# Moving one product of the second gate/up pair ahead, and fixing the place of the token scale's sum, in a float32 decoder layer on one core

## The chip, the cores and the metric

The kernel runs on one NeuronCore of a Trainium2 chip. The metric is device time in microseconds (us) for one execution, lower is better; the value given for a kernel is the median of several runs. One core works here, so no other core's work disturbs it.

## The reference

One hybrid decoder layer in float32, with 512 tokens, a model width of 2048 and 16 learned meta tokens in front. What the change touches is its last third:

```python
h = h + o @ w_out[l]                       # o: attention and convolution groups, each normalized
n2 = _rmsnorm(h, g_ffn[l])                 # one scale for each token, from the sum of h*h over 2048
h = h + (jax.nn.silu(n2 @ w_gate[l]) * (n2 @ w_up[l])) @ w_down[l]    # D_FF = 5632
```

`_rmsnorm` multiplies each token by `rsqrt(mean(h*h) + 1e-6)` and each channel by its gain.

## The kernel before, in words

Everything is stored transposed: channels on the 128 partitions, tokens along the free axis. A float32 product is made of three fp32r products: each operand is split into a high part (a cast on ScalarE, ACT) and a low part (a subtraction on VectorE, DVE), and hi·hi + hi·lo + lo·hi is summed in PSUM (L740 to L742 for the stage in question).

**The stages.** First come the input projection, attention and convolution, then the output projection `w_out` (16 output tiles, L821 to L902), then 44 *pairs* of gate and up tiles (`for f in range(FT)`, L972), then the down projection in four chunks. The change lies where `w_out` ends and the first two gate/up pairs run.

**A pair.** `pair_product` (L744) multiplies the activation, cut into 2 x 2 blocks (token halves by channel halves), with a 2 x 2 arrangement of weight blocks b11, b12, b21, b22 by Winograd's form of Strassen's scheme: seven block products instead of eight. Each product is 8 channel tiles times 3 passes, so 24 matmuls of 128x128 by 128x256. I call them slots 0 to 6:

| slot | weight | activation | PSUM bank |
|---|---|---|---|
| 0 | b11 | f0 | x |
| 1 | t1 = b11 + b12 | f1 | z |
| 2 | t2 = t1 + b22 | f2 | x |
| 3 | b22 | f3 | z |
| 4 | t3 = b12 + b22 | f4 | x |
| 5 | b21 (the product "a12 b21") | f5 | y |
| 6 | t2 + b21 | f6 | x |

"P1s5" below is slot 5 of the second pair, counted from 0. The pair P0 runs its slots in the order 5, 0, 1, 2, 3, 4, 6 (`FIRST_ORDER`, L663), because f5 is ready first; all other pairs run 0 to 6. The banks x, y and z exist twice, so two pairs can be open at once. Where products of different banks have no dependence, the scheduling layer mixes their matmuls, so PE's order is not quite the program's.

**Weights.** `prepare_pair` (L665) makes one split per product, in the order of use. `split_quad` (L639) casts the high part on ACT (L642) and makes the low part on DVE (L643), in a ring of three places of `sw_split`: the split for a product can begin when the product three before it is done. The same function makes the sums: t1 and t3 with `add_quads` (L649), t2 at L686, its last addition at L659 (`add_last`). Sums and raw blocks lie in six places of `sw_in`: places 0 to 3 hold the four loaded blocks, 4 and 5 hold t1/t2 and t3. Once a block is no more needed, the block of the same name of the next pair is loaded over it by SyncE's DMA queue (SP; `load_next`, L616, issued at L614). During `w_out` only places 0 to 3 are used (`load_wide`, L628).

**Activations.** Each finished `w_out` tile goes through `residual` (L835: two multiplications by token scales on DVE, two additions) and a copy with the FFN gain on ACT (L840); then the blocks f0 to f6 are mixed and split (L187, L188, L847 to L852). f0, f1, f2 and f5 stay in SBUF. f3, f4 and f6 find no room until `w_out`'s inputs are released, so they are gathered in DRAM and come back with six DMAs from GpSimd's queue (POOL, L884): f3 in two halves, f4 in two, f6 in two. Between f3's and f4's issues POOL adds the last tile's squares to `acc_h` (L207).

**The token scale of the FFN.** `token_scale` (L493) splits `acc_h`, sums it over the partitions by two products with a matrix of ones (L501 and L502, tile `ss_h`), adds and scales on DVE (L503), and takes the reciprocal root: logarithm and exponential on ACT (L194, L195), then four operations of a Newton step on POOL (L196 to L199), which write the scale back to `acc_h`. It is handed to pair 0 as `fourth` and called behind slot 3 (L773), at a high priority, so that the scheduling layer may move its instructions ahead. `gate` (L938) uses the scale on DVE: L941 for u, L943 for g.

Of the kernel before, what the change touches and what calls it, by code (L numbers as in the profile page):

```python
# [16 lines left out]
D = 2048  # L17
# [16 lines left out]
def hybrid_layer(ctx: ExitStack, tc: tile.TileContext, xT, w_in, w_out, w_gu, w_down, vecs, out):  # L34
# [9 lines left out]
    nc = tc.nc  # L44
    ve, sc, gp, pe = nc.vector, nc.scalar, nc.gpsimd, nc.tensor
# [48 lines left out]
    ones_r = keep.tile([P, P], F32R, name="ones_r")  # L94
# [125 lines left out]
    acc = accs[0]  # L220
# [269 lines left out]
    for h in range(HEADS):  # L490
        head(h)

    def token_scale(acc, dst, count, name, work, eng=ve):  # L493

        sh, sl, v, y, t = work
        split(sh, sl, acc, eng)
        ps = small(f"ss_{name}")  # L500
        pe.matmul(ps, ones_r, sh, start=True, stop=False)  # L501
        pe.matmul(ps, ones_r, sl, start=False, stop=True)  # L502
        ve.tensor_scalar(v, ps, 1.0 / count, EPS, ALU.mult, ALU.add)  # L503
        rsqrt(dst, v, SEQ, y, t, eng)
# [15 lines left out]
    for j in range(HEADS):  # L520
# [5 lines left out]
        y = t512(SEQ, "e2", 2)[:, :SEQ]  # L526
# [101 lines left out]
    def load_wide():  # L628

        i = len(wide)  # L630
        q = ORDER[(i + 2) % 4]
        if i < WIDE:
            wide.append(quad_place(0, q))
            nc.sync.dma_start(wide[i], w_out[OUT_TILES[1 + i // 2], i % 2])
        else:
            wide.append(None)
            load_quad(0, q)

    def split_quad(src, n):  # L639
        k = len(split_w) % (S_AHEAD + 1) * 2  # L640
        hi, lo = (w_place(sw_split, n, k + i) for i in range(2))
        sc.copy(hi, src)  # L642
        ve.tensor_tensor(lo, src, hi.bitcast(F32), ALU.subtract)  # L643
        split_w.append((hi, lo))
# [15 lines left out]
        load_next(i, "21")  # L660


    FIRST_ORDER = (5, 0, 1, 2, 3, 4, 6)  # L663

    def prepare_pair():  # L665
        if len(split_w) < WIDE:
            with tc.high_priority():
                split_quad(wide[len(split_w)], 8)
                load_wide()
            return  # L670
        i, s = divmod(len(split_w) - WIDE, 7)
        if i == len(pairs):
            return
        n = pairs[i][0]
        if i == 0:
            s = FIRST_ORDER[s]
        with tc.high_priority():
            b = {q: quads[i, q] for q in ("11", "12", "21", "22") if (i, q) in quads}
            if s == 0:
                split_quad(b["11"], n)  # L680
                add_quads(i, "t1", b["11"], b["12"])
                load_next(i, "11")
            elif s == 1:
                split_quad(sums["t1"], n)
                sums["t2"] = sums["t1"]
                ve.tensor_tensor(sums["t2"], sums["t2"], b["22"], ALU.add)  # L686
                if i:
                    add_t3(i, b)
            elif s == 2:
                split_quad(sums["t2"], n)  # L690
                if not i:
                    add_t3(i, b)
            elif s == 3:
                split_quad(b["22"], n)
                load_next(i, "22")
            elif s == 4:
                split_quad(sums["t3"], n)
            elif s == 5:
                split_quad(b["21"], n)
                if i:  # L700
                    add_last(i, b)
            else:
                if not i:
                    add_last(i, b)
                split_quad(sums["t2"], n)
                if i + 1 == SIX:
                    load_quad(SIX + 1, QUADS[1])
# [16 lines left out]
    def block_product(ps, act, start):  # L724

        prepare_ahead(1 + S_AHEAD)  # L730
        i = (used[0] - WIDE) // 7
        hi, lo = split_w[used[0]]
        used[0] += 1
        m = ps.shape[-1] // T2
        n = pairs[i][0] // m
        for j in range(m):
            p, skip = ps[:, j * T2 : (j + 1) * T2], m > 1 or not start
            for k in range(n):
                kk = slice((j * n + k) * P, (j * n + k + 1) * P)
                pe.matmul(p, hi[:, kk], act[:, 0, k], start=start and j == k == 0, stop=False, skip_group_check=skip)  # L740
                pe.matmul(p, hi[:, kk], act[:, 1, k], start=False, stop=False, skip_group_check=skip)  # L741
                pe.matmul(p, lo[:, kk], act[:, 0, k], start=False, stop=k == n - 1, skip_group_check=skip)  # L742

    def pair_product(acts, c1, c2, fourth=None):  # L744

        i, cols = (used[0] - WIDE) // 7, c1.shape[-1]

        def bank(name):
            return xyz.tile([P, 512], F32, tag=name, name=f"{name}{i}")[:, :cols]

        def side(name):
            n = {"p1": 0, "p5": 1, "u2": 2}[name]
            if cols == T2 or not n:
                return sides[:, n * T2 : n * T2 + cols]
            return c2[:, 2 - n]

        y, z, x = bank("y"), bank("z"), bank("x")  # L760
        p1, p5, u2 = side("p1"), side("p5"), side("u2")
        if not i:
            block_product(y, acts[5], True)
        block_product(x, acts[0], True)
        sc.copy(p1, x)
        block_product(z, acts[1], True)
        sc.copy(p5, z)
        block_product(x, acts[2], False)
        sc.copy(u2, x)
        block_product(z, acts[3], False)  # L770
        ve.scalar_tensor_tensor(c2[:, 0], z, -1.0, u2, ALU.mult, ALU.subtract)
        if fourth:
            fourth()  # L773
        block_product(x, acts[4], False)
        ve.scalar_tensor_tensor(c2[:, 1], x, -1.0, p5, ALU.mult, ALU.subtract)
        if i:
            block_product(y, acts[5], True)
        ve.tensor_tensor(c1[:, 0], y, p1, ALU.add)
        block_product(x, acts[6], False)
        return x  # L780
# [22 lines left out]
    acts = {}  # L803
# [3 lines left out]
    fx = {i: dram.tile([P, 2, 8, T2], F32R, name=f"fx{i}") for i in (3, 4, 6)}  # L807
    for _ in range(4):
        load_wide()

    def wide_tmp(tag, dt=F32, bufs=1):
        n_tmp[0] += 1
# [8 lines left out]
    for i, j in enumerate(OUT_TILES):  # L821
# [6 lines left out]
        ps = ps_out[i]  # L828
# [75 lines left out]
    acts = [acts[s] for s in range(7)]  # L904
# [211 lines left out]
```

## Time and profile before

| what | value |
|---|---|
| median of 3 runs | 2065.69 us (2063.52 to 2066.52) |
| the profiled execution | 2066.56 us |
| its span | 2064.8 us |
| TensorE (PE) busy | 2051.6 us |
| VectorE (DVE) busy | 1628.3 us |
| ScalarE (ACT) busy | 1016.9 us |
| GpSimd (POOL) busy | 369.3 us |
| gate/up pairs start on PE at | 792.69 us |

How to read it: times of the trace are microseconds from the span's start; the profiled execution's own time is 1.8 us more than its span. In a timeline each row is start, duration, engine, line, operation, output<-input, shape, count, and in brackets the engine's idle time before it and what ended that. Matmuls overlap by their pipeline, so a matmul's cost is the distance from its start to the next one's start, not its duration; the same holds in small for DVE and ACT. "PEclk" is the share of TensorE's full clock that was granted.

### The profile page before, as it was taken

To read this page: it belongs to the slowest core of one execution; us is meant where nothing else is said; L and a number is where in the kernel's file an instruction comes from. 1 tells how busy PE (TensorE), PEld (TensorE's weight loads), DVE (VectorE), ACT (ScalarE), POOL (GpSimd) and SP (SyncE) were. 2 spreads that over 40 slices of the span, in tenths; PEclk is the share of its full clock that TensorE was granted. 3 is DMA by queue.
4 is the path that set the end of the run, shared out by engine and by line. 5 is a ranking of instruction groups with operands and counts; after the bars stand their busy time and mean duration, and the time that the engine had idled before them with its cause. 6 is when DMAs were issued, how large, how long until landed. Compare 5 with 4: busy or idle time off the path is not lost.

```text
span 2064.8 us, 39370 instructions
## 1 busy us (share of the span) xinstructions
PE 2051.6 (99%) x16086; PEld 1977.9 (96%) x16086; DVE 1628.3 (79%) x2133; ACT 1016.9 (49%) x1522; POOL 369.3 (18%) x499
## 2 busy tenths in 40 slices
PE   9999999999999999999999999999999999999999
PEld 8899999999998888999999999999999999999999
DVE  7877767433336668999898898898888888888888
ACT  7666565322224334555455555555555544444443
POOL 0111111010103544111111111011011243121110
PEclk9999999999999999999999999999999999999999
DMA  5122222222335656546545555455455899798864
GB/s 198 63 81 74 81 72 83 82 93 94 98 107 168 187 178 229 159 138 194 169 136 176 159 152 172 148 172 161 147 175 155 256 332 348 195 293 213 217 150 94
DMA packets 144117, 330.41 MB, mean 160 GB/s; under 512 B 12400, under 2 KB 62064, under 8 KB 143936
## 3 DMA queue, kind: packets, MB, share of 16 engines
q1 hardware_dynamic: 67456, 212.50, 32.2%
q0 software_dynamic: 76480, 115.40, 21.8%
q8 instruction: 126, 2.06, 0.4%
q14 instruction: 55, 0.45, 0.1%
HBM read 260.74 MB, written 67.11 MB: 159 GB/s over the span
## 4 chain that ended last, share of the span: by engine, by line
PE 95%; DVE 2%; DMA 2%; ACT 1%; issue 0%; POOL 0%; DVEq 0%; POOLq 0%; ACTq 0%
PE x L740 11%; PE x L741 11%; PE x L742 11%; PE z L740 6%; PE z L741 6%; PE z L742 6%; PE y L742 3%; PE y L740 3%; PE y L741 3%; PE po L719 3%; PE po L721 3%; PE po L720 3%; PE pv L173 2%; PE pu L177 1%; PE pc L173 1%; PE pu L173 1%
## 5 line engine op out<-in xcount | busy, mean ns | idle before, releaser
L642 ACT CAST sw_split<-sw_in 128x1024 fp32r<-128x1024 f32 (+1 forms) x534 | 526.5, 987 | 553.0 <-PE z L741 166.2
L643 DVE TENSOR_TENSOR sw_split<-sw_in,sw_split 128x1024 fp32r<-128x1024 f32 (+1 forms) x534 | 614.6, 1151 | 97.4 <-ACT sw_split L642 94.2
L741 PE MATMUL x<-f,sw_split 128*128 128x256 f32 x1408 | 388.4, 276 | 2.9 <-DMA f<-fx 2.7
L740 PE MATMUL x<-f,sw_split 128*128 128x256 f32 x1408 | 388.5, 276 | 0.2 <-ACT f L187 0.2
L742 PE MATMUL x<-f,sw_split 128*128 128x256 f32 x1408 | 387.9, 276 | 0.0
L741 PEld LDWEIGHTS x<-f,sw_split 128*128 128x128 f32 x1408 | 265.1, 188 | 3.5 <-DMA f<-fx 3.1
L740 PEld LDWEIGHTS x<-f,sw_split 128*128 128x128 f32 x1408 | 265.0, 188 | 1.0 <-ACT f L187 0.4
L742 PEld LDWEIGHTS x<-f,sw_split 128*128 128x128 f32 x1408 | 265.0, 188 | 0.0
L142 DVE TENSOR_TENSOR wlo<-raw,whi 128x512 fp32r<-128x512 f32 (+1 forms) x198 | 139.7, 709 | 125.0 <-ACT whi L141 124.2
L932 POOL DMA_DIRECT2D fd<-s x147 | 103.9, 928 | 684.1 <-DVE s L188 667.6
L141 ACT CAST whi<-raw 128x512 fp32r<-128x512 f32 (+1 forms) x198 | 121.1, 614 | 180.8 <-PE pu L175 64.5
L741 PE MATMUL z<-f,sw_split 128*128 128x256 f32 x704 | 193.7, 275 | 0.2 <-DVE f L188 0.2
L740 PE MATMUL z<-f,sw_split 128*128 128x256 f32 x704 | 193.6, 275 | 0.0
L742 PE MATMUL z<-f,sw_split 128*128 128x256 f32 x704 | 193.6, 275 | 0.0
L649 DVE TENSOR_TENSOR sw_in<-sw_in 128x1024 f32<-128x1024 f32 (+1 forms) x144 | 164.5, 1142 | 4.6 <-DMA sw_in<-w_down 0.6
L742 PE MATMUL x<-ring,sw_split 128*128 128x256 f32 x608 | 167.3, 275 | 0.5 <-DVE sw_split L643 0.5
L740 PE MATMUL x<-ring,sw_split 128*128 128x256 f32 x608 | 167.2, 275 | 0.0
L741 PE MATMUL x<-ring,sw_split 128*128 128x256 f32 x608 | 167.2, 275 | 0.0
L741 PEld LDWEIGHTS z<-f,sw_split 128*128 128x128 f32 x704 | 132.2, 188 | 0.4 <-DVE f L188 0.4
L742 PEld LDWEIGHTS z<-f,sw_split 128*128 128x128 f32 x704 | 132.2, 188 | 0.0
L740 PEld LDWEIGHTS z<-f,sw_split 128*128 128x128 f32 x704 | 132.2, 188 | 0.0
L742 PEld LDWEIGHTS x<-ring,sw_split 128*128 128x128 f32 x608 | 114.1, 188 | 0.7 <-DVE sw_split L643 0.7
(345 smaller groups left out, 5255.9 us busy)
## 6 DMA issues: line engine op xcount, KB each, us to landing
sw_in<-w_gu SPq DMA_DIRECT2D x176, 512.0 KB, 4.1
raw<-w_in SPq DMA_DIRECT2D x92, 512.0 KB, 3.3
fd<-s POOLq DMA_DIRECT2D x147, 256.0 KB, 5.4
sw_in<-w_down SPq DMA_DIRECT2D x96, 384.0 KB, 4.1
ring<-fd POOLq DMA_DIRECT2D x42, 768.0 KB, 17.0
sw_in<-w_out SPq DMA_DIRECT2D x30, 512.0 KB, 3.6
out_T<-d POOLq DMA_DIRECT2D x54, 256.0 KB, 4.6
sw_in<-w_down SPq DMA_DIRECT2D x16, 512.0 KB, 7.8
```

Of the source, the lines that this page charges most:

```text
L141: sc.copy(hi[:, :c], raw)
L142: ve.tensor_tensor(lo[:, :c], raw, hi[:, :c].bitcast(F32), ALU.subtract)
L173: pe.matmul(ps, wh, ah[:, a:b], start=k == 0, stop=False)
L642: sc.copy(hi, src)
L643: ve.tensor_tensor(lo, src, hi.bitcast(F32), ALU.subtract)
L649: return ve.tensor_tensor(sums[name], a, b, ALU.add)
L719: pe.matmul(ps, hi[:, kk], ah, start=k == 0, stop=False)
L720: pe.matmul(ps, hi[:, kk], al, start=False, stop=False)
L740: pe.matmul(p, hi[:, kk], act[:, 0, k], start=start and j == k == 0, stop=False, skip_group_check=skip)
L741: pe.matmul(p, hi[:, kk], act[:, 1, k], start=False, stop=False, skip_group_check=skip)
L742: pe.matmul(p, lo[:, kk], act[:, 0, k], start=False, stop=k == n - 1, skip_group_check=skip)
L932: gp.dma_start(fd[c][s][:, :, k], t[:, :, i])
```

## The change

Pair 1's slot 5 (a12 b21) is made right behind pair 0's slot 5, so P0s5, P1s5, P0s0, P0s1, P0s2, P0s3, P0s4, P0s6, then P1s0 to P1s4 and P1s6; from pair 2 on the order is as before. Its y bank waits in the second y buffer until pair 1 adds it. Its weight block is loaded once more, early, into place 5 of `sw_in` (`load_early`, while `w_out` starts), since b21 of pair 1 is needed again for t2 + b21 and is loaded for that as before. So one 512 KB load is added, and no matmul, split or sum is added or dropped. Since place 5 is taken until P1s5's split, pair 0's sum t3, which goes there, comes behind that split. The second part: the first of the two products with ones of `ss_h` is kept in program order, behind P0s3.

```diff
-        pe.matmul(ps, ones_r, sh, start=True, stop=False)
+        first_sum = pe.matmul(ps, ones_r, sh, start=True, stop=False)
+        if in_order:
+            tc.keep_in_program_order(first_sum)
...
-    FIRST_ORDER = (5, 0, 1, 2, 3, 4, 6)
+    EARLY = 2
+    order_w = [(i, 5) for i in range(EARLY)] + [
+        (i, s) for i in range(len(pairs)) for s in range(7) if i >= EARLY or s != 5
+    ]
+
+    def load_early():
+        quads["early"] = w_place(sw_in, 8, 5)
+        nc.sync.dma_start(quads["early"], pairs[1][1][2])
...
-        if i == 0:
-            s = FIRST_ORDER[s]
+        i, s = order_w[len(split_w) - WIDE]
...
-                split_quad(b["21"], n)
-                if i:
+                split_quad(quads["early"] if i == 1 else b["21"], n)
+                if i >= EARLY:
                     add_last(i, b)
             else:
-                if not i:
+                if i < EARLY:
                     add_last(i, b)
                 split_quad(sums["t2"], n)
...
-        y, z, x = bank("y"), bank("z"), bank("x")
+        y, z, x = early.pop(i, None) or bank("y"), bank("z"), bank("x")
         if not i:
             block_product(y, acts[5], True)
+            early[1] = bank("y", 1)
+            block_product(early[1], acts[5], True)
         block_product(x, acts[0], True)
...
-        if i:
+        if i >= EARLY:
             block_product(y, acts[5], True)
...
     for _ in range(4):
         load_wide()
+    load_early()
...
-            token_scale(acc_h, acc_h, D, "h", (w[:, 0], w[:, 1], a[:, 0], a[:, 1], b), gp)
+            token_scale(acc_h, acc_h, D, "h", (w[:, 0], w[:, 1], a[:, 0], a[:, 1], b), gp, True)
```

More of the change, by code (lines that the diff above doesn't have):

```diff
@@ L491, in hybrid_layer, with token_scale @@
         head(h)
-    def token_scale(acc, dst, count, name, work, eng=ve):
+    def token_scale(acc, dst, count, name, work, eng=ve, in_order=False):
         sh, sl, v, y, t = work
@@ L670, in prepare_pair @@
             return
-        i, s = divmod(len(split_w) - WIDE, 7)
-        if i == len(pairs):
+        if len(split_w) - WIDE == len(order_w):
             return
+        i, s = order_w[len(split_w) - WIDE]
         n = pairs[i][0]
-        if i == 0:
-            s = FIRST_ORDER[s]
         with tc.high_priority():
@@ L730, in block_product @@
         prepare_ahead(1 + S_AHEAD)
-        i = (used[0] - WIDE) // 7
+        i = order_w[used[0] - WIDE][0]
         hi, lo = split_w[used[0]]
@@ L742, in block_product, with bank @@
                 pe.matmul(p, lo[:, kk], act[:, 0, k], start=False, stop=k == n - 1, skip_group_check=skip)
+    n_pair, early = [0], {}
     def pair_product(acts, c1, c2, fourth=None):
-        i, cols = (used[0] - WIDE) // 7, c1.shape[-1]
-        def bank(name):
+        i, cols = n_pair[0], c1.shape[-1]
+        n_pair[0] += 1
+        def bank(name, i=i):
             return xyz.tile([P, 512], F32, tag=name, name=f"{name}{i}")[:, :cols]
```

## The prediction

> **What bounds the kernel now.** I read the page first, then PE's waits around the change, then PE's timeline there, then the engines that release it.
>
> ```profile
> PE 2051.6 (99%) x16086; PEld 1977.9 (96%) x16086; DVE 1628.3 (79%) x2133; ACT 1016.9 (49%) x1522; POOL 369.3 (18%) x499
> ...
> L642 ACT CAST sw_split<-sw_in 128x1024 fp32r<-128x1024 f32 (+1 forms) x534 | 526.5, 987 | 553.0 <-PE z L741 166.2
> ```
>
> PE is busy for 99% of the span, so an edit pays only where PE really waits or runs slowly. PE's waits between 792 and 847 us (columns: total us, times, longest us):
>
> ```profile
> PE x L741 <- DMA f<-fx: 2.7, 2, 2.3
> PE y L742 <- DVE sw_split L643: 1.9, 1, 1.9
> ```
>
> Two waits: for f4 and f6 coming back from DRAM (2.3 and 0.4), and for the low part of P1s5's own split (1.9). Now PE's timeline; the rows are the starts of P0s5; P0s4 with its wait; the wait inside P0s6; P1s3; P1s5; and, as a mark I call M, the first matmul of P2s2 (slot 2 of pair 2). Up to M both kernels issue the same matmuls; from M on both have the same order in the built programs.
>
> ```profile
> 792.69 0.28 PE L740 MATMUL y<-f,sw_split 128*128 128x256 f32 x1
> ...
> 808.40 0.28 PE L740 MATMUL x<-f,sw_split 128*128 128x256 f32 x1
> 810.99 0.39 PE L741 MATMUL x<-f,sw_split 128*128 128x256 f32 x1 [2.32 <-DMA f<-fx]
> ...
> 818.47 0.39 PE L741 MATMUL x<-f,sw_split 128*128 128x256 f32 x1 [0.42 <-DMA f<-fx]
> ...
> 827.47 0.28 PE L740 MATMUL z<-f,sw_split 128*128 128x256 f32 x1
> ...
> 830.19 0.28 PE L740 MATMUL y<-f,sw_split 128*128 128x256 f32 x1
> ...
> 846.26 0.28 PE L740 MATMUL x<-f,sw_split 128*128 128x256 f32 x1
> ```
>
> P1s3 to P1s5 is 830.19 - 827.47 = 2.72 us: one product, 0.1133 a matmul. From P0s5 to M lie 16 products and the two of `ss_h` (0.23 each, estimated as twice 0.1133): 16 x 2.72 + 0.46 = 44.0 of work in 846.26 - 792.69 = 53.6 us. So 9.6 us are lost here, and that is the most the change could win. Where: 15.71 instead of 13.83 (five products and one of `ss_h`) up to P0s4: 1.9, small waits for f0 to f2; 2.5 between P0s4's first two matmuls; then a slow stretch:
>
> ```profile
> 813.00:815.00 2.00, 2.00 (x11) 2.00 (x11) 0.00 (x0) 0.00 (x0) 0.00 (x0) 0.50 1.13 422
> ```
>
> The granted clock is 0.50 here: 11 matmuls in 2 us instead of 18. It follows PE's 2.3 us of waiting, lasts about 3.4 us and so costs 1.7. Then 0.6 at 818.47, 2.1 at P1s5, and crumbs.
>
> **The change part by part.** I compare two limits at M: PE behind f6's landing, and DVE behind the token scale. The later one is the forecast.
>
> *PE behind f6.* f6's second half released PE at 818.47. In the old order PE then stood in P0s6 with 17 matmuls of P1s0 already done. In the new order P0s4, five matmuls of P1s0, then P0s6 follow each other, so at f6's landing 24 matmuls (P1s5) more and 12 of P1s0 fewer are done: 210 matmuls are left before M against 222. 210 x 0.1133 = 23.8, M at 842.3, if nothing else waits: **4.0 us** less. f4's wait goes (PE reaches P0s4 about 2.7 us of work later, f4 lands at 810.99), but what is late next is f6: PE arrives near 815.5 and waits until 818.5. The 2.3 us of waiting at f4 are thus mostly moved, not removed. P1s5's own wait of 2.1 goes, since that product was made long before.
>
> *Does f6 land when it did?* It is issued by POOL behind L207, and shares the DMA engines with SP's weight loads.
>
> ```profile
> 797.96 2.25 POOL L207 TENSOR_TENSOR acc_h<-acc_h,w 128x512 f32<-128x512 f32 x1 [3.34 <-ACT w L206]
> 800.16 2.88 POOL L884 DMA_DIRECT2D f<-fx  x4
> ...
> 824.59 2.14 POOL L199 TENSOR_TENSOR acc_h<-work_a,work_b 128x512 f32<-128x512 f32 x1
> ```
>
> ```profile
> f<-fx POOLq DMA_DIRECT2D x2, 1024.0 KB, 14.5
> ```
>
> ```profile
> DMA packets 1396, 5.10 MB, mean 399 GB/s; under 512 B 95, under 2 KB 95, under 8 KB 1396
> ```
>
> ```profile
> 789.32 3.65 SPq L614 DMA_DIRECT2D sw_in<-w_gu  x2
> ```
>
> L207 waits for the last tile's residual on DVE. Its timeline:
>
> ```profile
> 786.99 2.30 DVE L649 TENSOR_TENSOR sw_in<-sw_in 128x1024 f32<-128x1024 f32 x1
> ...
> 791.41 1.21 DVE L643 TENSOR_TENSOR sw_split<-sw_in,sw_split 128x1024 fp32r<-128x1024 f32 x1
> 792.96 0.69 DVE L836 TENSOR_TENSOR w<-po,acc_a 128x512 f32<-128x512 f32 x1 [0.34 <-PE po L721]
> 793.57 0.68 DVE L838 TENSOR_TENSOR w<-po,acc_c 128x512 f32<-128x512 f32 x1
> ...
> 798.65 0.42 DVE L849 SCALAR_TENSOR_TENSOR src<-src 128x256 f32<-128x256 f32 x1
> 799.10 1.39 DVE L851 SCALAR_TENSOR_TENSOR src<-src 128x256 f32<-128x256 f32 x1
> ...
> 807.74 1.21 DVE L649 TENSOR_TENSOR sw_in<-sw_in 128x1024 f32<-128x1024 f32 x1
> 808.87 1.21 DVE L643 TENSOR_TENSOR sw_split<-sw_in,sw_split 128x1024 fp32r<-128x1024 f32 x1
> ...
> 836.67 1.23 DVE L643 TENSOR_TENSOR sw_split<-sw_in,sw_split 128x1024 fp32r<-128x1024 f32 x1
> ```
>
> At 791.41 stood P0s0's split; in the new order P1s5's stands there, and t3's sum, which ran at 786.99 in idle time, comes behind it, since P1s5's block occupies its place. A sum or a split of 128x1024 takes 808.87 - 807.74 = 1.13 us. So L836 starts at 791.41 + 2 x 1.13 = 793.7 instead of 792.96, and L207 and the issues of f4 and f6 come 0.7 later. SP's load of P1's b12 (789.32, released by t3's sum) moves to 793.7, that of b11 (the second issue of that row, 792.6, released by P0s0's split) to about 796.7: 1.0 MB falls among f3's transfers. At 399 GB/s that is 2.6 us at most if nothing gives way; against it P1's b21 and b22 load later, and P2's b11 no longer ahead of f6's end (0.5 MB, 1.3 us sooner). Bounds for f6's landing: 1.3 earlier to 0.7 + 2.6 = 3.3 later; I take no shift, in the middle of them, because the engines move the same bytes by the same end.
>
> *DVE behind the token scale.* In the old run the second product of `ss_h` starts at 816.60:
>
> ```profile
> L502 PE MATMUL ss_h<-work_r,ones_r x1: 401/401/401, 816.6 to 816.6; 128*128 128x512 f32 x1
> L503 DVE TENSOR_SCALAR work_a<-ss_h x1: 683/683/683, 817.7 to 817.7; 128x512 f32<-128x512 f32 x1
> ```
>
> L503 follows at 817.7. POOL's last step, L199 above, ends at 824.59 + 2.14 = 826.7, so 10.1 after it; the low part of P2s0 follows on DVE at 836.67. In the new order the second product stands 9 matmuls behind P0s3's end. When does P0s3 end? PE's own pace gives 792.69 + 6 x 2.72 = 809.0. But the splits are late: behind the residual (0.75 later) come P0s1's low part, then t2's sum (which was ahead of it), then P0s2's. In order: L836 793.7, two more of 0.6 (793.57 - 792.96), P0s0's low part 1.13 to 796.6, L839 to 797.2, then the copy with the gain on ACT:
>
> ```profile
> 796.62 0.73 ACT L840 ACTIVATE src<-w,vec 128x512 f32<-128x512 f32 x1 [2.91 <-DVE w L839]
> ```
>
> That makes 798.0, and the six mixing operations that follow on DVE, 0.34 each (the distance to the next start is less than the 0.42 shown), end at 800.1. A DVE operation beside POOL's L207 is held up: 799.10's took 1.39, its sibling before it 0.42. The cost of that is 0 to 1.0; I take 1.0.
>
> So P0s1's low part is made from 801.2 to 802.3; PE wants it at 792.69 + 3 x 2.72 + 0.23 = 801.1 and waits 1.2. f2's low part 0.34, t2's sum 1.13: 803.8; ACT's cast of t2 (987 ns in the mean, first row above) to 804.8, low part to 806.0: PE, which could begin P0s2 at 804.9 and use the low part 0.23 later, waits 0.9 more. P0s3 ends near 811.3, or 812.2 if POOL holds up one more operation; both waits lie ahead of the f6 wait, which hides them from PE's limit. The second product of `ss_h` is then at 811.3 to 812.2 plus 1.25: 813.0, 3.6 earlier than now. DVE's L503 is queued behind P1s0's low part, up to 815.2, so 2.2 behind the product instead of 1.1; the chain from L503 to POOL's end, 826.7 - 817.7 = 9.0, gives 824.2.
>
> L941 waits there for the scale, and behind it on DVE stand, up to and with P2s0's low part, eight splits and sums of 1.13, four operations of 0.60 and two of 0.34: 12.1 us, 836.3. That is two splits or sums more than in the old order, where P1s5's split stood behind the scale but three others stood ahead of it. P2s0's third matmul, the first to use that low part, therefore starts at 836.3, and 70 matmuls later is M: 836.3 + 7.9 = 844.2, **2.0 us** earlier than 846.26. This is the later limit, so the forecast.
>
> *Other edits.* The extra 512 KB load is issued at the start of the `w_out` stage:
>
> ```profile
> sw_in<-w_out SPq DMA_DIRECT2D x30, 512.0 KB, 3.6
> ```
>
> Loads like it land in 3.6 us while the product pair that consumes two of them takes 10.9 (48 matmuls of 0.23); if that cover were gone it would cost 0.5 MB at 399 GB/s, 1.3. Ordering the first product with ones behind P0s3 removes no matmul; its cast on ACT is made earlier than needed. Nothing after M changes place, and I find no wait of PE there that grows with an earlier arrival.
>
> The Trainium skill's page "TensorE: Matmul & The Clock Gate", section "HAM oscillation — how this bites in real kernels", warns of idle gaps of more than about 3.4 us. Here a wait of 2.3 us was followed by the halved clock, so the trace shows it for shorter ones. By the page the new f6 wait of about 3 would leave the clock alone, and rival 1 below would keep its whole 4.0; by the row it can halve the clock, and rival 1 keeps 2.3.
>
> **The rivals.**
>
> *1. DVE is not the later limit.* If POOL's chain ends 2 us sooner, only PE's limit counts: 4.0 us less. For it: PE, not DVE, is 99% busy. Against: L941 blocks everything behind it on DVE. A halved clock behind the f6 wait would take 1.7 of it (2.3 left); in the forecast it would hide under DVE's limit, 842.3 + 1.7 = 844.0 against 844.2.
>
> *2. f6 lands later.* With 3.3 us later, PE's limit is 845.6: 0.7 less than before. For it: the engines are busy through 803 to 816. Against: the same bytes in all.
>
> *3. Slower: the token scale comes later, not earlier.* Place: P0s1 and P0s2, where PE waits for splits twice in 5 us. If that halves the clock (1.7) and POOL holds up two more DVE operations (1.0 each), the second `ss_h` product moves by 3.7, and M with it: 844.2 + 3.7 = 847.9, 1.7 slower. It decides from 2.0 us of extra lateness at P0s3's end. For it: DVE has no idle time from 791 to 811. Against: 2.3 us in one piece was needed for the one halving seen.
>
> **How the numbers follow.** The sum stands against the profiled execution, 2066.56: 2066.56 - 2.0 = 2064.6. The median of the runs is 2065.69, 0.87 lower, so the forecast for a median is 2065.69 - 2.0 = 2063.7. Chances: forecast (1 to 3 less) 0.45; rival 1 (3 to 4.5 less, 2061.7 at 4.0) 0.20; rival 2 (0 to 1 less, 2065.0) 0.17; rival 3 (up to 3 more, 2067.4) 0.18. The range 2061.2 to 2066.8 reaches from just past rival 1 to the milder half of rival 3; about 0.05 is left out below and 0.12 above. A measurement of this kernel can tell about 0.2%, 4.1 us, from no change. Faster by that is the far end of rival 1 (0.07); slower by that is the far end of rival 3, with a second halving of the clock (0.04); within it lies the rest, 0.89.
>
> **What would show it.** Right: no wait for f4 at P0s4, one wait of 2 to 3.5 us for f6 in P0s6, small waits for splits at P0s1 and P0s2, second `ss_h` product near 813, POOL's L199 ending near 824, DVE idle ahead of L955 (the old L941), a short wait at P2s0. Wrong: f6 released before 816 or after 820; `ss_h` after 815; PE waiting after M where it did not; more than 5 us between the two kernels' distance from P0s5 to M.

## The result, and the profile after

The changed kernel takes 2066.66 us (median of 22 runs, 2066.06 to 2069.16), the kernel before, run beside it, 2064.31 (22 runs, 2062.82 to 2066.52). The ratio is 1.0013 with a 95% interval of 1.0007 to 1.0019: about 2.4 us slower, where 2.0 less was forecast. The forecast time of 2063.7 stood on the median of three runs, 2065.69; the 22 runs put the kernel before 1.4 lower.

The profiled execution of the changed kernel is the slowest of its 22: 2069.16 us, span 2067.5. PE's share and the costliest group on its page are what they were:

```profile
PE 2051.9 (99%) x16086; PEld 1978.5 (96%) x16086; DVE 1627.6 (79%) x2133; ACT 1017.0 (49%) x1522; POOL 368.4 (18%) x499
...
L644 ACT CAST sw_split<-sw_in 128x1024 fp32r<-128x1024 f32 (+1 forms) x534 | 526.7, 988 | 551.2 <-PE z L749 163.2
```

PE's waits between 785 and 850 us (total, times, longest):

```profile
PE x L748 <- ACT sides L778: 2.7, 1, 2.7
PE x L750 <- DVE sw_split L645: 2.2, 2, 1.8
PE z L750 <- DVE sw_split L645: 1.1, 1, 1.1
```

No wait for f4 or f6 is left. In their place PE waits 2.7 us for a *copy on ACT*, and for splits. PE's timeline shows where: P0s1's low part, P0s2's first matmul, the first product with ones, P1s2's low part.

```profile
803.24 0.38 PE L750 MATMUL z<-f,sw_split 128*128 128x256 f32 x1 [1.07 <-DVE sw_split L645]
...
808.70 0.39 PE L748 MATMUL x<-f,sw_split 128*128 128x256 f32 x1 [2.66 <-ACT sides L778]
...
815.93 0.39 PE L501 MATMUL ss_h<-work_r,ones_r 128*128 128x512 f32 x1
...
829.80 0.39 PE L750 MATMUL x<-f,sw_split 128*128 128x256 f32 x1 [1.79 <-DVE sw_split L645]
```

P0s2 adds into bank x, and ACT's copy of p1 (L778) must have read that bank first. ACT's timeline tells why the copy is late:

```profile
804.75 1.05 ACT L644 CAST sw_split<-sw_in 128x1024 fp32r<-128x1024 f32 x1 [1.95 <-DVE sw_in L694]
806.82 0.62 ACT L187 CAST work_r<-acc_h 128x512 fp32r<-128x512 f32 x1 [1.02 <-DMA f<-fx]
807.34 1.04 ACT L644 CAST sw_split<-sw_in 128x1024 fp32r<-128x1024 f32 x1
808.29 0.37 ACT L778 COPY sides<-x 128x256 f32<-128x256 f32 x1
```

Ahead of the copy stand P0s2's cast, then the cast of `work_r` for the token scale, which itself waits 1.0 for a DMA, then P0s3's cast. In the old order the copies of p1 and p5 stood ahead of `work_r`. DVE's timeline where the scale arrives:

```profile
827.92 0.69 DVE L955 TENSOR_TENSOR u<-u,acc_h 128x512 f32<-128x512 f32 x1 [1.90 <-POOL acc_h L199]
828.53 1.22 DVE L645 TENSOR_TENSOR sw_split<-sw_in,sw_split 128x1024 fp32r<-128x1024 f32 x1
```

P1s2's split stands behind L955, and L955 waits for the scale: that is the wait at 829.80. The clock in two windows of this execution:

```profile
810.00:812.00 2.00, 2.00 (x11) 0.50 1.19 401
830.50:832.50 2.00, 2.00 (x11) 0.50 0.05 6
```

It is halved twice, each time behind one of these waits, while the trace of before that the prediction was made from has one halved stretch, and its 2066.56 us lie above all 22 runs of that kernel. So both kernels were traced once more.

**The kernel before again** (no edit).

> The kernel before once more, for a second trace of it. The first trace had one halving of the clock, behind the wait for f4, and was the slowest of its three runs. Theory C (that halving made the token scale and so P1s5's split late, and the kernel before is faster without it): in a trace without a halving at that place, the second product with ones starts near 815, the wait at P1s5 is shorter than 1 us or gone, and from P0s5 to M pass 51 to 52 us instead of 53.6. If f6's landing alone sets the pace, M comes at 53 us or more with or without the halving.

2064.06 us, span 2062.4, clock 1.000 throughout. P0s5 starts at 792.73, M is at 843.90: 51.17 us, where the first trace had 53.57. The two rows, and its waits between 785 and 850:

```profile
792.73 0.28 PE L740 MATMUL y<-f,sw_split 128*128 128x256 f32 x1
...
843.90 0.28 PE L740 MATMUL x<-f,sw_split 128*128 128x256 f32 x1
```

```profile
PE x L741 <- DMA f<-fx: 1.4, 1, 1.4
PE x L741 <- DVE f L188: 1.3, 1, 1.3
PE x L740 <- DMA f<-fx: 1.2, 1, 1.2
PE y L742 <- DVE sw_split L643: 0.9, 1, 0.9
PE x L740 <- ACT f L187: 0.2, 1, 0.2
```

PE doesn't wait for f4 at all here; it waits for f6's two halves (1.2 and 1.4), and the token scale is early:

```profile
820.78 1.31 POOL L199 TENSOR_TENSOR acc_h<-work_a,work_b 128x512 f32<-128x512 f32 x1
```

POOL ends at 822.1, 4.6 us sooner than in the trace that the prediction used: the second product with ones comes 2.3 sooner (814.3), and L198 and L199 take 0.62 and 1.31 us where they took 1.47 and 2.14 with DVE working beside them. L941, at 825.37, doesn't wait for the scale; in the first trace, at 827.74, it didn't either.

**The changed kernel again** (no edit).

> The changed kernel once more, for a trace in which perhaps no stretch is halved. If the halved clock alone made the changed kernel late at M, then without a halved stretch the distance from P0s5 to M is 51.2 us or less, as in the second trace of the kernel before (51.17). If the wait for p1's copy and the late token scale make it, the distance is 51.5 to 52.5 without a halved stretch and 1.7 more for each one, and P0s2 still starts 15 us or more behind P0s5, with a wait of 2 us or more for the copy.

2066.51 us, span 2064.8, clock 1.000 throughout; P0s5 at 792.61, M at 845.99: 53.38 us. So the loss is there without any halved clock: 53.38 - 51.17 = 2.2 of the 2.35 between the medians. Its waits between 785 and 850; on PE the rows of P0s2, the second product with ones, P2s0's low part and M; on DVE L955 and the split that P2s0 waits for:

```profile
PE x L750 <- DVE sw_split L645: 2.5, 2, 1.8
PE x L748 <- ACT sides L778: 2.4, 1, 2.4
PE z L750 <- DVE sw_split L645: 1.1, 1, 1.1
PE z L748 <- ACT sides L780: 1.0, 1, 1.0
```

```profile
807.71 0.38 PE L748 MATMUL x<-f,sw_split 128*128 128x256 f32 x1 [2.38 <-ACT sides L778]
...
814.59 0.40 PE L504 MATMUL ss_h<-work_r,ones_r 128*128 128x512 f32 x1
...
837.71 0.39 PE L750 MATMUL x<-f,sw_split 128*128 128x256 f32 x1 [0.77 <-DVE sw_split L645]
...
845.99 0.28 PE L748 MATMUL x<-f,sw_split 128*128 128x256 f32 x1
```

```profile
825.28 0.69 DVE L955 TENSOR_TENSOR u<-u,acc_h 128x512 f32<-128x512 f32 x1 [1.91 <-POOL acc_h L199]
...
836.43 1.22 DVE L645 TENSOR_TENSOR sw_split<-sw_in,sw_split 128x1024 fp32r<-128x1024 f32 x1
```

In kernels with added lines the numbers behind L777 are up to five higher. Below, "M" is always the distance from P0s5's start to the first matmul of P2s2. Theory A: ACT's order (the copy behind the `work_r` cast) delays P0s3 and with it the scale, and DVE's work queued behind the scale sets M. Theory B: f6's landing sets M in the changed kernel too, and the waits only stand in for it. Theory C: the halved clock alone is the loss; the trace just shown ends it.

### The profile page after: what moved, and what is told of

The parts are those of the page before. It is cut to its first block, busy times and chain, and to the rows that moved or that the text cites. A ratio compares the mean times of both kernels' runs of the same rounds, so it can differ in the third digit from the quotient of the medians.

```text
span 2067.5 us, 39371 instructions
## 1 busy us (share of the span) xinstructions
PE 2051.9 (99%) x16086; PEld 1978.5 (96%) x16086; DVE 1627.6 (79%) x2133; ACT 1017.0 (49%) x1522; POOL 368.4 (18%) x499
## 4 chain that ended last, share of the span: by engine, by line
PE 94%; DVE 2%; issue 1%; ACT 1%; DMA 1%; POOL 1%; SPq 0%; DVEq 0%; POOLq 0%; ACTq 0%
PE x L750 11%; PE x L749 11%; PE x L748 11%; PE z L749 6%; PE z L750 6%; PE z L748 6%; PE y L749 3%; PE y L748 3%; PE y L750 3%; PE po L727 2%; PE po L729 2%; PE po L728 2%; PE pv L173 2%; PE pu L177 1%; PE pc L173 1%; PE pu L173 1%
## 5 line engine op out<-in xcount | busy, mean ns | idle before, releaser
L651 DVE TENSOR_TENSOR sw_in<-sw_in 128x1024 f32<-128x1024 f32 (+1 forms) x144 | 164.5, 1142 | 4.7 <-DMA sw_in<-w_down 0.8
```

The costliest lines, as they stand in the source:

```text
L651: return ve.tensor_tensor(sums[name], a, b, ALU.add)
```

## The experiments

**One part at a time.** The first kernel is the changed one without the kept order of the product with ones, the second the old one with it:

```diff
-            token_scale(acc_h, acc_h, D, "h", (...), gp, True)
+            token_scale(acc_h, acc_h, D, "h", (...), gp)
```

> The changed kernel without the second part: the first product with ones is not kept in program order. In the built order ACT's cast of acc_h (work_r) then stands behind the copies of P0s0's and P0s1's results again, where the kernel before has it; the order of the products on PE is that of the changed kernel. Theory A (the loss is ACT waiting in the changed kernel at that cast for a DMA, with the copy that P0s2 needs behind it): PE's wait of 2.7 us for ACT at P0s2 goes, P0s2 starts 2 to 3 us earlier, from P0s5 to the mark M about 52 us instead of 55.3, and the kernel is within 1 us of the one before (ratio 0.9990 to 1.0005). Theory B (the loss is DVE, since one split and the sum t3 now stand ahead of the residual): the waits at P0s1 and P0s2 stay about as long, and the ratio stays at 1.001 or above.

2070.36 us, ratio 1.0030 (1.0019 to 1.0042); M 56.11, with 6.8 us at half clock. PE's row:

```profile
805.80 0.79 PE L501 MATMUL ss_h<-work_r,ones_r 128*128 128x512 f32 x1 [2.31 <-ACT work_r L187]
```

The expectation had the cast in another place. Without the kept order the first product with ones lands in the middle of P0s1, and PE itself waits 2.3 us for the cast, which stands on ACT behind P0s2's cast and ahead of the copy of p1 (805.13 against 806.60); here it waits for no DMA. So the second part is worth 2070.36 - 2066.66 = 3.7 us once the first is made, and the cast's early place on ACT comes from the first part, not the second.

> The kernel before with the second part alone: the first product with ones kept behind P0s3. On ACT nothing moves in the built order, on PE only the first product with ones, by 31 matmuls; the second stays where it was. Theory A and B both expect no change (ratio 0.9997 to 1.0003), since the second product starts the token scale. If the second part costs by itself, on PE, it is slower by its 1 to 2 us here.

2064.57, ratio 1.0001 (0.9992 to 1.0010): by itself the second part does nothing that the runs could tell.

**The cast behind the copies.** The changed kernel, with the scale's instructions on ACT queued behind p5's copy instead of behind the last load:

```diff
-        sc.copy(p5, z)
+        p5_copy = sc.copy(p5, z)
...
-        with tc.high_priority(1 << 20), tc.issue_after(last_f.ins):
+        with tc.high_priority(1 << 20), tc.issue_after(p5_copy.ins):
```

> The changed kernel with the token scale's instructions held back until the copy of P0s1's result is issued, so that on ACT the cast of acc_h stands behind both copies, and the two products with ones stand together behind P0s3. Theory A (ACT's queue): PE's wait for ACT at P0s2 shrinks from 2.7 us to at most 1.5, since only P0s3's cast stands ahead of the copy, P0s2 starts about 1.5 us sooner after P0s5 than the 15.4 us of the changed kernel, and M follows 51 to 52.5 us after P0s5; ratio to the kernel before 0.9995 to 1.0006. Theory D (what costs is the first pair's scaling of u on DVE, which waits for the token scale with P1s2's split behind it): P0s2 starts sooner, but P1s2 still waits 1.5 us or more, since that scaling now stands even ahead of P1's t2 sum on DVE; M at 52.5 us or later, ratio 1.0005 to 1.0015.

2066.87, ratio 1.0012 (1.0003 to 1.0022). P0s2's wait falls to 1.0, `ss_h`'s second product comes at 812.97 instead of 814.59, and POOL's L199 ends at 821.8 instead of 825.2. M is 52.85 with one stretch at half clock. But now PE waits for f6 (1.0 at 818.04), and 2.1 at P1s2 for the copy of p1 there. DVE:

```profile
821.80 0.69 DVE L955 TENSOR_TENSOR u<-u,acc_h 128x512 f32<-128x512 f32 x1 [3.28 <-POOL acc_h L199]
822.41 1.22 DVE L694 TENSOR_TENSOR sw_in<-sw_in 128x1024 f32<-128x1024 f32 x1
823.55 1.22 DVE L651 TENSOR_TENSOR sw_in<-sw_in 128x1024 f32<-128x1024 f32 x1
```

With the scale due earlier, the scheduling layer put L955 ahead of pair 1's two sums, and DVE stands idle for 3.3 us with work behind it. The scale came 3.4 us sooner, and DVE had no more done for it.

**What the cast waits for.** The changed kernel without the store of the last residual tile (that output tile is left out):

> The changed kernel without the store of the last residual tile to the output (the DMA on SP's queue behind two weight loads); its tile of the output is left out. ACT's order is that of the changed kernel, with the cast of acc_h ahead of the copies. Theory A, with the DMA named: the cast no longer waits until 806.8 but starts when its place on ACT comes up, near 805.8; P0s3's weight cast and the copy follow 1 us sooner, P0s2 starts 1 us sooner than in the changed kernel, and the kernel gains about 1 us on it (ratio 1.0005 to 1.0010). If the cast waits for something else (its engine, POOL's sum), nothing changes, ratio 1.0010 to 1.0015.

2065.92, ratio 1.0007 (0.9997 to 1.0016), M 52.76 with one halved stretch. The `work_r` cast no longer waits, and P0s2's wait falls from 2.4 to 1.5. In the next kernel (e5), with the store in place, the trace puts the same wait down to that store:

```profile
805.99 0.62 ACT L187 CAST work_r<-acc_h 128x512 fp32r<-128x512 f32 x1 [0.55 <-DMA out_T<-w]
```

The rest of the copy's lateness is the two casts ahead of it.

**The first multiplication of u on POOL**, in the changed kernel, in e3's, and in the kernel before:

```diff
-            ve.tensor_tensor(u1, u1, r_h, ALU.mult)
+            (ve if f else gp).tensor_tensor(u1, u1, r_h, ALU.mult)
```

> The changed kernel with the first pair's multiplication of u by the token scale (L955) on POOL instead of DVE, all else equal. Theory D: DVE no longer waits there with P1s2's split behind it, PE's wait of 1.8 us (2.1 between starts) at P1s2 goes below 0.5, ratio about 1.0003 (0.9997 to 1.0008). Theory A alone: P0s2's wait for ACT of 2.7 us stays as it is in both cases, and the rest of the loss, about half, stays.

2069.19, ratio 1.0025 (1.0015 to 1.0035), M 53.94 with one stretch at half clock. No gain: P1s2 waits 2.7 for p1's copy, which on ACT now stands behind the activation of g (826.17); that waits 2.5 for DVE's multiplication of g, and this one for the scale. DVE's queue was relieved and ACT's took its place.

> Both edits at once: the cast behind the copies and the scaling of u on POOL. If A and D are two separate waits, both go, M follows 50 to 51 us after P0s5, and the kernel is faster than the one before: ratio 0.9985 to 0.9998. If f6's landing sets the pace after all, M is at 51 us or more and the ratio 0.9998 to 1.0003.

2065.69, ratio 1.0007 (0.9997 to 1.0016), M 51.40. At M 2.0 of the 2.2 us are gone, by the ratio about half of the loss; the interval no longer excludes the time of the kernel before.

> The kernel before with the first pair's scaling of u on POOL, as a control for the two runs with that edit. Its wait of 0.9 us at P1s5 goes or shrinks; M at 50 to 51 us after P0s5; ratio 0.9993 to 1.0001. If it gains as much as the changed kernel does by the same edit, the edit says nothing of the change.

2064.43, ratio 1.0001 (0.9992 to 1.0010), M 51.12: in the old order it is worth nothing that the runs could tell; the scale isn't late there (L941 waited for it in neither trace).

**p1's copy ahead of the next weight's cast**, on top of e6 and, without the edit on POOL, on top of e3:

```diff
-        sc.copy(p1, x)
+        with tc.high_priority(1 << 20 if i < EARLY else 0):
+            sc.copy(p1, x)
```

> The changed kernel with the two edits of e6 (the cast for ss_h behind the copies, and the first multiplication of u on POOL) and with the copy of p1 on ACT ahead of the cast of the next weight for the first two pairs. If the copies' places in ACT's queue are what is left of the loss, the waits for L778 at P0s2 (1.0) and at P1s2 (1.3) go, M comes 49.5 to 50.5 us behind P0s5 and the ratio is 0.9990 to 1.0000. If f6 sets the pace, the wait for f6 grows by the 1.0 that P0s2 gains, only P1s2's 1.3 is won, and the ratio is 0.9995 to 1.0005.

2065.58, ratio 1.0006 (0.9997 to 1.0015), M 51.60. No product waits for a copy, and nothing is won: P0s2 starts sooner and f6 is waited for (1.0), as theory B says, but then P2s0's low part is late by 1.5, as theory A says.

> The kernel of e3 with the copy of p1 on ACT also ahead of the next weight's cast, for the first two pairs; the multiplication of u stays on DVE. If ACT's queue is what is left after e3, the waits for the copy (1.0 at P0s2, 2.1 at P1s2) go, M comes 50.5 to 51.5 us behind P0s5, no halved stretch, ratio 0.9998 to 1.0007. If DVE's block behind the scale is (3.3 us of DVE idle ahead of L955 in e3, with two sums of pair 1 queued behind it), P1s2 waits 1 us or more for its split in place of the copy, M comes 51.5 or later, and the ratio is 1.0005 to 1.0015.

2065.66, ratio 1.0006 (0.9997 to 1.0015), M 51.85. Of the waits for the copy 0.4 is left, at P1s2; P2s0's low part is late by 1.4.

**Is f6's landing set by its issue?** In the old order, and on top of e11, POOL issues all six loads before it adds the last tile's squares:

```diff
-                square_sum(acc_h, hj, False, wide_tmp("s"))
...
+            with tc.high_priority(1 << 20), tc.issue_after(last_f.ins):
+                square_sum(acc_h, hj, False, wide_tmp("s"))
```

> The kernel before, with one edit: POOL issues all six loads of f3, f4 and f6 and only then adds the last tile's squares (L207). If f6's landing sets the pace of the old order, f4 and f6 land 1.5 to 3 us sooner, the waits for f4 and f6 go, M comes 49 to 50 us behind P0s5 instead of 51.2, and the ratio is 0.9985 to 0.9995. If the token scale sets it (DVE blocked behind its last step), L207 and the second product of ss_h come no sooner, M does not move, and the ratio is 0.9995 to 1.0005, with a new wait for a split of pair 1 in place of the one for f6.

2064.52, ratio 1.0001 (0.9992 to 1.0009), M 51.79. The four loads of f4 and f6 are issued from 794.5 to 797.4 instead of from 799.5 on, five microseconds sooner, and f6 still releases PE at 817.57 (817.14 in the second trace of before). From 800 to 814 us the DMA queues move (last column, GB/s):

```profile
800.00:814.00 14.00, 12.24 (x102) 1.00 1.13 408
```

In the same stretch the second trace of before moves 395 GB/s: an earlier issue hardly adds bytes to this stretch and mostly spreads the same ones. That half of the expectation was wrong: the issue doesn't move f6's landing. A later one doesn't either: in e3, e6, e11, e14, e17 and e19 the second half of f6 is issued only at 809.9 to 810.6, and f6 releases PE at 817.3 to 818.0.

> The kernel of e11 with the edit of e9: POOL issues all six loads before L207. If f6's landing is the last limit once the copies are in place, f6 lands 1.5 to 3 us sooner, its wait goes, M comes 48 to 49 us behind P0s5, and the ratio is 0.9980 to 0.9993. If the token scale is, ss_h comes later by L207's delay (up to 2 us), the wait moves to a split of pair 1 or pair 2, and the ratio is as that of e11 or up to 0.0007 above it.

2067.75, ratio 1.0016 (1.0007 to 1.0025), M 53.83: the scale comes 2.7 later than in e11, and the wait moves to P1s3 (0.9 for a copy, 1.0 for a split), with a stretch at half clock behind it. The loads don't delay L207, which runs at 798.74 here and at 799.27 in e11. It is the cast of `work_r` that got another place on ACT, here and in e11:

```profile
812.90 0.61 ACT L187 CAST work_r<-acc_h 128x512 fp32r<-128x512 f32 x1
```

```profile
807.98 0.63 ACT L187 CAST work_r<-acc_h 128x512 fp32r<-128x512 f32 x1
```

In e9 it moved too, from 804.28 (second trace of before) to 813.64, and the scale came 3.7 later. So the times of these two kernels can't be put down to the order of the loads alone.

**The scale not waited for.** The two multiplications by the scale for pair 0 are left out (its u and g stay unscaled), in the changed kernel, in e3's and in the kernel before. This also takes two operations of 0.6 us off DVE.

```diff
-        if f < 2 * CHUNKS[0]:
+        if 0 < f < 2 * CHUNKS[0]:
...
-        ve.tensor_tensor(g1, g1, r_h, ALU.mult)
+        if f:
+            ve.tensor_tensor(g1, g1, r_h, ALU.mult)
```

> The changed kernel without the two multiplications by the token scale for pair 0 (L955 and L957; u and g of the first pair are left unscaled), so that neither DVE nor, behind it, ACT stands waiting for POOL's L199 before pair 1's splits. If the late scale costs what the rows of the waits say, P1s2's wait for its split (1.9) and P1s3's for the copy of z (1.2) go, the one for p1's copy at P0s2 (2.4) stays, M comes 50.3 to 50.8 us behind P0s5 instead of 53.38, and the ratio is 0.9995 to 1.0003. If those waits only stand in for another limit behind f6, M comes 52.5 or later and the ratio stays at 1.0008 or more.

M 51.65, 1.7 less than the changed kernel's 53.38, and between the two expectations. The time is not: 2066.75 in the median, ratio 1.0012 (1.0003 to 1.0021), as the second expectation has it. In 8 of its 11 runs the mean clock was below 1.000; the three others, the traced one among them, took 2064.79 to 2065.56. That the 2.2 us that P0s2 still waits bring the halved clock is likely, but no trace of such a run was taken. The old order gains 0.7 at M by the same edit (e16, below), so of the 2.2 us lost at M the scale accounts for 1.0, and 1.2 stay.

> The kernel of e3 (the cast for ss_h behind the copies) without the two multiplications by the scale for pair 0 (left unscaled). With both queues free only f6's landing is left of the limits named: f6 releases PE at 817.5 to 818.5, 210 matmuls of 0.1133 later is M, so 48.1 to 49.1 us behind P0s5 (2 to 3 less than the kernel before), ratio 0.9985 to 0.9993. If DVE's own amount of work sets P2s0's split (at 836.3 in e6 and e11), M comes 50.3 to 51.4 behind P0s5 and the ratio is 0.9997 to 1.0006.

2063.79, ratio 0.9997 (0.9988 to 1.0006), M 49.83. M is again between the two, where 210 matmuls behind f6 without a wait would have been 49.1 at most; the ratio is that of the second expectation.

> The kernel before without the two multiplications by the scale for pair 0 (left unscaled), as the control of the two others. The scale was no limit in the old order if the trace without a halved stretch reads rightly: only the wait at P1s5 (1.0) can go, M comes 50.0 to 51.2 behind P0s5, and the ratio is 0.9994 to 1.0002. If the forecast's reading was right and DVE behind the scale set M in the old order, M comes 2 us or more sooner and the ratio is 0.9991 or less.

2063.08, ratio 0.9992 (0.9983 to 1.0000), M 50.45. M is at 843.02, 25.27 us behind f6's release:

```profile
817.75 0.39 PE L741 MATMUL x<-f,sw_split 128*128 128x256 f32 x1 [1.69 <-DMA f<-fx]
```

222 matmuls of 0.1133 are 25.15: without these two multiplications the old order runs from f6 to M without a wait, bound by f6 alone. With them (second trace of before) M came 26.76 behind f6's release, 1.6 more, of which 1.1 pass at P1s5, whose split is late. So in the old order too DVE sets M in part, though L941 doesn't wait for the scale.

Of the two orders with no scale to wait for, the new one is ahead by 50.45 - 49.83 = 0.6 at M. That is not the order's gain:

```profile
817.40 0.39 PE L749 MATMUL x<-f,sw_split 128*128 128x256 f32 x1 [0.79 <-DMA f<-fx]
...
842.84 0.28 PE L748 MATMUL x<-f,sw_split 128*128 128x256 f32 x1
```

In e14 f6 released PE 24.39 behind P0s5, in e16 25.18 behind it, 0.8 later. From f6 to M the new order took 25.44 and the old one 25.27: the 12 matmuls fewer (1.4 us) are lost again, mostly at P1s3, for a copy, and at P2s0, for a split. And e14 takes 0.7 more than e16 in all: in these two traces its P0s5 starts 0.4 later and 0.8 is lost behind M (about 0.25 of it ahead of P2s4).

**The version the experiments point to.** e17 with L955 kept behind pair 1's sums on DVE:

```diff
-        t3 = add_quads(i, "t3", b["12"], b["22"])
+        t3 = sums["t3_add"] = add_quads(i, "t3", b["12"], b["22"])
...
-            ve.tensor_tensor(u1, u1, r_h, ALU.mult)
+            if f:
+                ve.tensor_tensor(u1, u1, r_h, ALU.mult)
+            else:
+                with tc.issue_after(sums["t3_add"].ins):
+                    ve.tensor_tensor(u1, u1, r_h, ALU.mult)
```

> The kernel of e17 with the multiplication of u by the scale (L955) kept behind pair 1's two sums on DVE, so that DVE makes them while it waits for L199. If DVE's block behind the scale is what is left, this comes close to e14, where the scale isn't waited for at all (M 49.83 behind P0s5, 2063.79): M 49.8 to 50.8, ratio 0.9995 to 1.0003, level with the kernel before or a little better. If DVE's amount of work is the limit, P2s0's split stays at 836 and M at 51.4 or later, ratio 1.0004 or more.

2066.03, ratio 1.0008 (0.9999 to 1.0017), M 51.25. No gain on the kernel before. Six of the 11 runs had a mean clock below 1.000 (2065.18 to 2067.46 us); the five others took 2064.71 to 2066.03. DVE around the scale and at P2s0's split:

```profile
817.96 2.20 DVE L694 TENSOR_TENSOR sw_in<-sw_in 128x1024 f32<-128x1024 f32 x1
820.08 1.63 DVE L651 TENSOR_TENSOR sw_in<-sw_in 128x1024 f32<-128x1024 f32 x1
822.91 0.69 DVE L960 TENSOR_TENSOR u<-u,acc_h 128x512 f32<-128x512 f32 x1 [1.20 <-POOL acc_h L199]
823.52 1.22 DVE L645 TENSOR_TENSOR sw_split<-sw_in,sw_split 128x1024 fp32r<-128x1024 f32 x1
...
834.07 1.21 DVE L645 TENSOR_TENSOR sw_split<-sw_in,sw_split 128x1024 fp32r<-128x1024 f32 x1
```

From L960 on DVE is never idle up to P2s0's split, and PE uses that at 835.34, 12.4 us behind L960. In the changed kernel it is 837.71 - 825.28 = 12.4 too, again without a gap on DVE. So DVE's amount of work behind the scale is the limit of the new order, in the changed kernel and in the mended one. In e6, e11 and e17 P2s0 waits for its low part too (0.8, 1.5, 1.4).

## Why the prediction was wrong, point by point

Two steps failed. The old order's M, against which the 2.0 us were counted, was 2.4 too late: 53.57 in one slow execution, 51.17 in a typical one. And the path to the scale left out ACT's copy out of bank x: PE waited 2.4 us for it at P0s2, not 0.9 for a split, which made the scale late and, with somewhat more time behind it, the new order's M 1.9 later than forecast.

- **What M was measured against: wrong, 2.4 us.** "9.6 us are lost here, and that is the most the change could win." 2.4 of these were this one execution's: in the second trace, with the clock at full speed, the old order is at M after 51.17, not 53.57, f4 isn't waited for, and L199 ends at 822.1, not 826.7; five traces of the old order and its variants (b2, e2, e7, e9, e16) have M after 50.45 to 51.79. The halved clock is not all of it: the wait for f4 came ahead of it. The prediction saw the halved stretch, priced it at 1.7, and still let the new order win it. It allowed 0.87 for the span's being above the median of three runs. The forecast's own M for the new order, 844.2 - 792.69 = 51.5, was 0.3 *behind* the old order's 51.17.
- **"PE, which could begin P0s2 at 804.9 [...] waits 0.9 more": wrong, 1.5 us.** P0s1's wait came as forecast (1.07 against 1.2), with one DVE operation held up beside L207 (1.53 us, against 1.0 more that was taken). At P0s2 the prediction followed the split and not the bank: x has to be copied by ACT first, and ACT's queue had the `work_r` cast and another cast ahead of that copy. PE waited 2.4 (2.7 in the first trace). e3 moves the cast of `work_r` and the wait falls to 1.0; e11 and e17 put the copy ahead of the other cast too, and the wait for the copy is gone.
- **The cast "is made earlier than needed": wrong.** Its price was put at nothing. Its place comes with the first part of the change (e1). It is what stands ahead of the copy, and e1 shows the same cast stopping PE for 2.3.
- **The second `ss_h` product at 813.0, L199's end at 824.2: late by 1.6 and 1.0** (814.59 and 825.24 in the second trace), as the later P0s3 gives. In the profiled execution the product is at 817.2, past the 815 that the prediction named as a sign against it.
- **"This is the later limit": right.** 12.1 from the scale to P2s0's low part were forecast, 12.4 measured, in the changed kernel and in e19; the 7.9 from there to M became 8.3. Together with the later scale: 1.0 + 0.3 + 0.4, and 0.1 from P0s5's start, make the 1.9 between 51.5 and 53.38. With the `work_r` cast behind the copies e6, e11, e17 and e19 are at M after 51.25 to 51.85, near the forecast's 51.5, though not always by its sum: in e17 the scale is 2.7 sooner than forecast, and two sums more stand behind it (14.7 from the scale to P2s0 in place of 12.1).
- **Waits at P1s2 and P1s3: not forecast.** The prediction counted DVE's queue only as far as P2s0. P1s2's split stands directly behind L955 and is late first (1.8). With DVE's tail behind them these waits cost nothing of their own as long as P2s0 still waits (0.8).
- **f6: landing right, wait gone.** No shift was taken; f6 released PE between 816.8 and 818.1 in eleven traces (818.47 was forecast), the one with the earlier issue among them. The 2 to 3.5 us wait forecast there was 0, since PE came late, and 0.8 to 1.1 in e3, e6, e11, e14, e17 and e19.
- **The rivals.** Rival 1 fell: DVE was the later limit. Rival 2 didn't occur. Rival 3 had the sign, the place (P0s1 and P0s2) and the way (a later scale), at 0.18; its price was of other things: no halved clock and no POOL delay was needed, but a copy on ACT.
- **Sum.** Forecast -2.0, measured +2.35: 4.35 apart, of which 2.4 is the base and 1.9 the new order's M. The time of 2066.66 lay in the range, near its upper end; that is luck, since the median that the range stood on was 1.4 too high.

What stays open: why 0.3 to 0.9 us more pass behind M in the kernels with the new order than in the old one (1.4 in e1, nothing in e4; about 0.25 of it ahead of P2s4 in e6, e11, e14, e17 and e19), and so why e6, e11 and e17, at M within 0.2 to 0.7 of the old order, still take 1.2 to 1.6 us more.

## What to carry to other kernels

Before a wait is priced as a prize, look whether the trace is typical: with a stretch at half clock in it, the loss behind it belongs to that execution, and the same kernel traced again may not have it. A product waits for its bank as well as for its operands, so follow every in-order queue that must read or empty the bank (here ACT's copies) when an edit moves other work ahead in it. And moving work ahead of a block (the scale) helps only the engine that is the limit there: here it left 12 matmuls fewer behind f6 and put two more of DVE's splits and sums behind the scale.

## What the runs showed of the hardware

**The clock is halved after waits of about 2 us, and not every time.** A halved stretch lasted 3.4 us in each trace that has one, and 6.8 in e1. Counting the timed runs whose mean granted clock was below 1.000, beside PE's longest wait in the kernel's trace: e14 (1.1 us) 0 of 11, e2 (1.3) 0 of 11, e6 (1.3) 1 of 10, e7 (1.4) 0 of 10, e17 (1.4) 3 of 11, e11 (1.5) 4 of 11, e19 (1.5) 6 of 11, e9 (1.6) 4 of 11, e16 (1.7) 2 of 11, e4 (2.0) 5 of 11, e3 (2.1) 8 of 10, e15 (2.2) 8 of 11, e1 (2.3) 6 of 6, e5 (2.7) 9 of 10; the changed kernel (2.4 and 2.7) 13 of 22, and none in its second trace. Where in the kernel the clock fell is known for the traced executions alone. e13 stands apart: two waits of 0.9 and 1.0 within 1.5 us, and 10 of 11. The Trainium skill's page "TensorE: Matmul & The Clock Gate", section "HAM oscillation — how this bites in real kernels", puts the point at idle gaps of more than about 3.4 us. No wait here was that long, so the measurement decides: with waits of 2.0 to 2.7 us the clock fell in most runs (49 of 70 together), though not in all.

**POOL and DVE slow each other, both ways.** In e17 the sums L694 and L651 run after POOL's chain, in e19 beside it. e17, DVE and then POOL:

```profile
822.18 1.22 DVE L694 TENSOR_TENSOR sw_in<-sw_in 128x1024 f32<-128x1024 f32 x1
```

```profile
819.53 0.61 POOL L198 TENSOR_SCALAR work_b<-work_b 128x512 f32<-128x512 f32 x1
820.23 1.31 POOL L199 TENSOR_TENSOR acc_h<-work_a,work_b 128x512 f32<-128x512 f32 x1
```

e19, POOL:

```profile
816.92 2.15 POOL L197 TENSOR_TENSOR work_b<-work_b,work_a 128x512 f32<-128x512 f32 x1
819.17 1.47 POOL L198 TENSOR_SCALAR work_b<-work_b 128x512 f32<-128x512 f32 x1
820.72 2.15 POOL L199 TENSOR_TENSOR acc_h<-work_a,work_b 128x512 f32<-128x512 f32 x1
```

L694 takes 2.20 beside POOL instead of 1.22, L198 and L199 together 1.7 more: of the 3.3 us of DVE's idle time that e19 fills, 1.3 come back as a later scale (L199 ends at 822.87 instead of 821.54). The rows look as if the two took turns: L694 (to 820.16) ends 1.1 behind L197's end, L198 (to 820.64) 0.5 behind L694's, L651 (to 821.71) 1.1 behind L198's, and L199 (to 822.87) 1.2 behind L651's, each near its own undisturbed time. The Trainium skill's page "SBUF — State Buffer", section "Who interferes with whom", says that a DVE instruction with two SBUF inputs contends with a GpSimd instruction that reads SBUF; the rows agree.
